# Weight sums of matmul pairs in one piece and in place, three buffers for split weights, and every pair's weights split two products ahead

## The chip, the core and the metric

The kernel runs on one core of one Trainium2 chip. The metric is the device time of one execution in microseconds (us). The engines are named as the profile names them: PE is TensorE's matmul, PEld its weight load, DVE VectorE, ACT ScalarE, POOL GpSimd, SP SyncE, which here only issues DMAs.

## The reference

The reference is one decoder layer on 512 prompt tokens and 8 sample tokens, 520 columns together, with a model width of 2048: adaLN modulation, two token mixers (mLSTM and forgetting attention), sigmoid gates that merge them, an output projection, and a feed-forward block with a causal convolution of width 3. Nearly all of its work is these dense products:

```python
h = modulate(rmsnorm(x, norm1_w), sh1, sc1)
... = jnp.split(h @ w_in + b_in, SPLIT_POINTS, axis=-1)
merged = jax.nn.sigmoid(ga) * (y_m @ w_proj_a) + jax.nn.sigmoid(gb) * (y_f @ w_proj_b)
x = x + g1 * (merged @ w_out)
h2 = modulate(rmsnorm(x, norm2_w), sh2, sc2)
a, g = jnp.split(h2 @ w_ffn_in, 2, axis=-1)
out = (jax.nn.gelu(conv(a)) * g) @ w_ffn_out
```

## The kernel before

Everything is float32 at the interface. A weight tile of 128 x 1024 is loaded into a buffer `raw` by SP (`wraw`, L158) and then split into two float32r tiles: `wh`, the rounded value, by a cast on ACT, and `wl`, the remainder, by a subtraction on DVE (`wtwo`, L167 to L177). The features are split in the same way into high and low. A product of weights and features is then three matmuls: high with high, high with low, low with high (`three_of`, L240).

Two kinds of stages use this. In a **dense stage** (`dense`, L205) one output chunk of 128 channels is computed with 48 or 96 matmuls, and the scheduler sets the order of the instructions by priorities. In a **pair stage** (`Pair`, L254 to L335) two output chunks and two halves of the 520 columns are computed together with seven products instead of eight, by sums of weight quarters and of feature quarters. A quarter is named by (output chunk, half of the 2048 inputs). Four products take a sum of quarters as weights; the sums are called 1 to 4 (`total`, L275): 1 is (1,0)+(1,1), 2 is sum 1 and (0,0), 4 is sum 2 and (0,1), 3 is (0,0) and (1,0). Each product is 24 matmuls of 128 x 128 weights with 260 columns and accumulates into a PSUM tile `x`, `y` or `z`. The products come in the order 1, 5, 6, 3, 7, 2, 4 (ORDER, L252), for the first pair of the output projection in the order 1, 3, 6, 5, 7, 2, 4 (ORDER1).

Pairs run in four stages: 11 pairs of gates and 4 of attention values (`GatePair`, `ValuePair`, about 530 to 835 us), 8 pairs of the output projection (`WoPair`, about 1320 to 1485), 41 of the feed-forward input (`FfnPair`, about 1580 to 2410) and 2 times 8 of its output (`FoPair`, from about 2490 and 2720). Around the last two stand a stage in which the features are made while the first weights run (about 1485 to 1580) and two stages `Whole` with plain products (about 2410 to 2490 and 2640 to 2720).

In a pair stage the program order is fixed on PE, DVE and ACT (`Ordered`, L53): `run_pairs` (L337) goes product by product. Before product number r of a pair it takes out the result of the product before, lets the pair make sums and splits for later products (`ahead(r)`, L303), lets the next pair do the same if its turn has come, and then issues the 24 matmuls. SP's loads run ahead of that order as far as buffers come free.

The buffers: 8 tiles `raw`; `wh` and `wl` with two tiles each in the pool `wp`, and from the end of the stage before the output projection a third each in the pool `cf`, which every third split takes (`turn`, `more`, L164 to L170). A sum of quarters lies in two tiles `sw` of 128 x 512 from the small pool `p` (`pt`, L93), so a sum is two additions and a split of a sum is two casts and two subtractions. With `early` 1 (the gate and value pairs) a quarter is split in two pieces as well, and a split stands one product ahead of its use; with `early` 2 (the other stages) a quarter is split in one piece and splits stand two products ahead. The adaLN sums are kept in a tile `ads` (`ada_out`, L421).

Of the kernel before, what the change touches and what calls it, by code (L numbers as in the profile page):

```python
# [63 lines left out]
def tile_hybrid_step(ctx: ExitStack, tc: tile.TileContext, I, O):  # L64
# [90 lines left out]
    def raw_tile():  # L155
        return wp.tile([P, 1024], F32, tag="raw", name=nm("raw"), bufs=8)

# [5 lines left out]

    turn = [0]  # L164
    more = []
# [12 lines left out]

    def wsplit(src, raw=None):
        with tc.high_priority():  # L180
            return wtwo([raw or wraw(src)], src.shape[1])

# [71 lines left out]
    class Pair:  # L254

        def __init__(self, rows, X, order, early):
            self.rows, self.X, self.order, self.early = rows, X, order, early
            self.w, self.s, self.made = {}, {}, []  # L260
            self.uses = {(0, 0): 3, (1, 0): 2, (0, 1): 2, (1, 1): 2, 1: 2, 2: 2, 3: 1, 4: 1}
# [4 lines left out]

        def pieces(self, x):
# [5 lines left out]
            return [u[:, :512] for u in t] if isinstance(x, int) else [t[:, :512], t[:, 512:]]  # L273

        def total(self, n):  # L275

            if n in self.made:
                return
            self.made.append(n)
            a, b = {1: ((1, 0), (1, 1)), 2: (1, (0, 0)), 4: ((0, 1), 2), 3: ((0, 0), (1, 0))}[n]  # L280
            out = []
            for u, v in zip(self.pieces(a), self.pieces(b)):
                t = pt("sw")
                V.tensor_tensor(t[:, :512], u, v, op=ALU.add)
                out.append(t)
            self.s[n] = out

        def split(self, n):
            src = {1: (0, 0), 2: (0, 1), 4: (1, 1), 5: 1, 6: 2, 3: 4, 7: 3}[n]
            whole = None if isinstance(src, int) or self.early == 1 else self.s[src]  # L290
            halves = self.pieces(src)
            self.w[n] = wtwo(halves if whole is None else [whole], 1024)

# [42 lines left out]

    def run_pairs(units, early, late, start=None):  # L337
        loads = {2: {1: ((0, 0),), 2: ((1, 0), (1, 1)), 5: ((0, 1),)},
                 1: {1: ((0, 0),), 3: ((1, 0), (1, 1)), 5: ((0, 1),)}}[early]
        for t in range(-early if start is None else start, 7 * len(units) + 5):  # L340
            u, r = divmod(t, 7)
            now, nxt = (units[v] if 0 <= v < len(units) else None for v in (u, u + 1))
            if 0 <= u - 1 < len(units):
                units[u - 1].after(r + 7)
            if now:
                if r > 0:
                    now.take(now.order[r - 1])
                now.ahead(r)
            if nxt:
                if r in loads and now:  # L350
                    nxt.load(*loads[r])
                if r >= 7 - early:
# [275 lines left out]
    square(1)  # L628
    turn[0] += 1
    w_first = [wp.tile([P, 1024], F32R, tag=t, name=nm(t)) for t in ("wh", "wl")]  # L630
# [98 lines left out]
    def next_group():  # L729
        if raws:  # L730
            raw, k = raws.pop(0)
            ready.append(wtwo([raw], k * NPH * P))

# [535 lines left out]
    class GatePair(Pair):  # L1269
        def __init__(self, gates):  # L1270
            self.gates = gates
            super().__init__([I["w_in"][49 + g] for g in gates], hX, ORDER, 1)

# [45 lines left out]
    class ValuePair(GatePair):  # L1319
        def __init__(self, heads):  # L1320
            self.heads = heads
            self.chunks = [25 + 3 * hh + 2 for hh in heads]
            Pair.__init__(self, [I["w_in"][i] for i in self.chunks], hX, ORDER, 1)

# [64 lines left out]
    run_pairs(units, 1, {}, 0)  # L1389
    hX = units = t = None  # L1390
# [411 lines left out]
    class WoPair(AddPair):  # L1802
        which = G1

        def __init__(self, c):
            super().__init__([I["w_out"][c + e] for e in range(2)], mX, ORDER if c else ORDER1, 2)
            self.c = c
# [57 lines left out]
    for n, j in enumerate(order):  # L1865
# [22 lines left out]
        if n == KC - 1:  # L1888
            more.append(cf)
            turn[0] = 0  # L1890
            with tc.high_priority():
                units[0].split(1)
                units[0].total(1)
                units[0].total(2)
                units[0].total(4)
                turn[0] = 2
                units[0].split(3)
# [29 lines left out]
    def parts2(u, o, e):  # L1927
        return wtwo([raws.pop((u, o, e))], 1024)

    def cast2(u, o, e):  # L1930

        turn[0] += 1
        wh, wl = ((cf if turn[0] % 3 == 0 else wp).tile([P, 1024], F32R, tag=t, name=nm(t)) for t in ("wh", "wl"))
        raw = raws.pop((u, o, e))
# [41 lines left out]
    def first_weights(o):  # L1976
# [3 lines left out]
    r2 = st("rr")  # L1980
    run_pairs(units, 2, {
        0: lambda: (m_sums(7, 0), m_sums(7, 1)), 1: lambda: (m_parts(7, 5), m_sums(7, 2)),
# [205 lines left out]
    class FfnPair(Pair):  # L2188
        def __init__(self, f):
            super().__init__((I["w_fi"][f], I["w_fi"][KF + f]), X, ORDER, 2)  # L2190
            self.f = f
# [27 lines left out]
    class Whole:  # L2219
# [21 lines left out]
        def split(self, c):  # L2241
            if c < KC:
                self.w[c] = wtwo([self.raw.pop(c)], NR * P)

# [114 lines left out]
    class FoPair(AddPair):  # L2359
        which = G2  # L2360

        def __init__(self, c, f0, fX):
            super().__init__([I["w_fo"][c + e][:, f0 * P:(f0 + 16) * P] for e in range(2)], fX, ORDER, 2)
            self.c, self.end = c, f0 + 16 == KF
# [66 lines left out]
    for k in range(0, KC, 2):  # L2431
# [7 lines left out]
    pairs1, pairs2 = units_of(whole[0], NR), units_of(whole[1], KF // 2 + NR)  # L2439
    run_pairs(units, 2, {-2: lambda: eight(2, 1, 1, (0, 1), w), -1: lambda: whole_copy(2),  # L2440
                         1: lambda: sum_parts(7), 2: lambda: whole_conv(2), 3: lambda: sum_parts(4),
                         4: lambda: whole_gate(2),
                         **g2, **whole[0].begin(7 * len(units))})
# [3 lines left out]
    units, last = pairs1  # L2447
    run_pairs(units, 2, {**rest_of(whole[0], units, last), **whole[1].begin(7 * len(units))})
    units, last = pairs2
    run_pairs(units, 2, rest_of(whole[1], units, last))  # L2450
    cf.release()
# [96 lines left out]
```

## Time and profile before

| | us |
|---|---|
| three timed runs | 2862.55, 2864.59, 2865.11 |
| their median | 2864.59 |
| the profiled execution: span from its first to its last instruction | 2875.7 |

The profiled execution gives no time besides its span; the span is 11.1 us (0.4%) longer than the median of the timed runs. All rows further down come from this one profiled execution, and positions in it are counted in us from its first instruction. In the page, "busy" is the time in which an engine had at least one instruction under way; matmuls overlap, so a busy PE need not be a PE at its peak.

### The profile page before, as it was taken

Reading aid. Unit: us, or ns where it says so; the run is one execution under the profiler, and the core shown is the slowest. Engines: PE = TensorE matmul, PEld = TensorE weight load, DVE = VectorE, ACT = ScalarE, POOL = GpSimd, SP = SyncE. Lnnn points to the kernel's source line nnn. Section 1 sums busy time; section 2 is a strip of 40 time slices with the busy share of each in tenths; the row PEclk is TensorE's granted clock in tenths of the full one; section 3 lists DMA queues with packets and bytes.
Section 4 is the critical chain, followed back from the end, with each engine's and each line's share of the span. In section 5 each row is a group of like instructions: output and inputs, shape, how many; then the busy total and the mean of one; then the engine's idle time right before and its main releaser. Section 6 shows DMA issues by size and latency. Waiting matters only on the chain.

```text
span 2875.7 us, 58597 instructions
## 1 busy us (share of the span) xinstructions
PE 2845.9 (99%) x23462; PEld 2734.9 (95%) x23462; DVE 2165.4 (75%) x4016; ACT 1379.1 (48%) x2451; POOL 363.6 (13%) x649
## 2 busy tenths in 40 slices
PE   8999999999999999999999999999999999999999
PEld 6899998999998989799999999999999999999999
DVE  5987754677855667368888888888888887787787
ACT  4346643455544554335555544444444445544543
POOL 0001101221101123302111000000000001100100
PEclk9999999999999999999999999999999999999999
DMA  9934458745456676657763444444443437746752
GB/s 340 313 130 142 141 164 300 246 151 170 148 166 222 208 243 231 209 186 230 221 202 104 128 137 144 144 138 151 135 152 114 149 111 201 191 153 186 204 159 89
DMA packets 214298, 514.23 MB, mean 179 GB/s; under 512 B 24512, under 2 KB 77232, under 8 KB 214024
## 3 DMA queue, kind: packets, MB, share of 16 engines
q1 hardware_dynamic: 177232, 416.07, 44.8%
q0 software_dynamic: 36352, 94.18, 10.9%
q8 instruction: 184, 3.01, 0.4%
q14 instruction: 90, 0.74, 0.1%
q10 hardware_dynamic: 440, 0.23, 0.0%
HBM read 440.47 MB, written 66.46 MB: 176 GB/s over the span
## 4 chain that ended last, share of the span: by engine, by line
PE 89%; issue 4%; DVE 3%; DMA 2%; ACT 2%; POOL 0%; SPq 0%; ACTq 0%; POOLq 0%; DVEq 0%
PE x L60 31%; PE y L60 16%; PE z L60 8%; PE fi L221 7%; PE gate L221 4%; PE fo L60 3%; PE pa L221 3%; PE pre L60 3%; PE mo L221 2%; PE adp L417 2%; PE mv L221 2%; PE adp L60 1%; DMA ar<-in_w_ada 1%; PE mq L221 1%; PE mk L221 1%
## 5 line engine op out<-in xcount | busy, mean ns | idle before, releaser
L60 ACT CAST wh<-sw 128x512 fp32r<-128x512 f32 x638 | 365.7, 621 | 246.2 <-PE z L60 74.2
L60 DVE TENSOR_TENSOR wl<-sw,wh 128x512 fp32r<-128x512 f32 x638 | 411.2, 686 | 86.8 <-ACT wh L60 83.9
L60 PE MATMUL x<-bf,wh 128*128 128x260 f32 x2624 | 475.9, 282 | 0.2 <-DVE tg L60 0.2
L60 ACT CAST wh<-raw 128x1024 fp32r<-128x1024 f32 (+2 forms) x350 | 316.7, 917 | 296.3 <-PE x L60 132.8
L60 DVE TENSOR_TENSOR wl<-raw,wh 128x1024 fp32r<-128x1024 f32 (+2 forms) x350 | 365.8, 1056 | 123.0 <-ACT wh L60 110.5
L60 PEld LDWEIGHTS x<-bf,wh 128*128 128x128 f32 x2624 | 403.4, 188 | 0.4 <-issue 0.4
L60 PE MATMUL x<-bf,wl 128*128 128x260 f32 x1312 | 369.8, 282 | 0.0
L176 DVE TENSOR_TENSOR wl<-raw,wh 128x1024 fp32r<-128x1024 f32 (+1 forms) x115 | 139.5, 1213 | 192.4 <-ACT wh L175 178.9
L60 PEld LDWEIGHTS x<-bf,wl 128*128 128x128 f32 x1312 | 246.9, 188 | 0.0
L60 PE MATMUL y<-bf,wh 128*128 128x260 f32 x1312 | 239.3, 283 | 0.0
L175 ACT CAST wh<-raw 128x1024 fp32r<-128x1024 f32 (+1 forms) x115 | 119.5, 1040 | 216.1 <-issue 42.9
L60 DVE TENSOR_TENSOR sw<-raw,raw 128x512 f32<-128x512 f32 x316 | 203.1, 683 | 0.0
L60 PEld LDWEIGHTS y<-bf,wh 128*128 128x128 f32 x1312 | 201.9, 188 | 0.0
L60 PE MATMUL x<-ff,wh 128*128 128x260 f32 x1024 | 186.5, 283 | 0.0
L60 PE MATMUL y<-bf,wl 128*128 128x260 f32 x656 | 185.1, 282 | 0.0
L60 PEld LDWEIGHTS x<-ff,wh 128*128 128x128 f32 x1024 | 157.8, 188 | 0.0
L60 PE MATMUL x<-ff,wl 128*128 128x260 f32 x512 | 144.6, 282 | 0.0
L60 PE MATMUL x<-hf,wh 128*128 128x260 f32 x720 | 131.4, 283 | 0.0
L60 PE MATMUL fo<-fe,wh 128*128 128x260 f32 x768 | 125.6, 284 | 1.6 <-DVE fo L60 1.1
L60 PEld LDWEIGHTS y<-bf,wl 128*128 128x128 f32 x656 | 123.4, 188 | 0.0
L60 PE MATMUL z<-bf,wh 128*128 128x260 f32 x656 | 120.3, 284 | 0.0
L60 PEld LDWEIGHTS x<-hf,wh 128*128 128x128 f32 x720 | 110.7, 188 | 0.0
(641 smaller groups left out, 7586.9 us busy)
## 6 DMA issues: line engine op xcount, KB each, us to landing
raw<-in_w_fi SPq DMA_DIRECT2D x176, 512.0 KB
raw<-in_w_in SPq DMA_DIRECT2D x155, 512.0 KB
ar<-in_w_ada SPq DMA_DIRECT2D x192, 256.0 KB
raw<-in_w_ada SPq DMA_DIRECT2D x96, 512.0 KB
raw<-in_w_fo SPq DMA_DIRECT2D x64, 512.0 KB
raw<-in_w_out SPq DMA_DIRECT2D x32, 512.0 KB
raw<-in_w_fo SPq DMA_DIRECT2D x32, 384.0 KB
dff<-cc POOLq DMA_DIRECT2D x44, 260.0 KB
```

Of the source, the lines that this page charges most:

```text
L60: return lambda *a, **k: self.tc.keep_in_program_order(getattr(self.eng, op)(*a, **k))
L175: S.copy(wh[:, o], t[:, :m])
L176: V.tensor_tensor(wl[:, o], t[:, :m], wh[:, o].bitcast(F32), op=ALU.subtract)
L221: T.matmul(acc[:, z, :HN], a[:, o], b[:, z * HN:(z + 1) * HN], start=(k == 0 and i == 0), stop=(k == K - 1 and i == 2))
L417: ins = T.matmul(ps[32 * g:32 * g + 32, :], cs[:, k, :], w, start=first, stop=last, tile_position=(0, 32 * g))
```

## The change

1. A sum of quarters is one addition of 128 x 1024 into one tile of the pool `raw`. Sum 3 is written over the quarter (1,0); with ORDER, sums 2 and 4 are written over the sum that they are made from. With ORDER1 sums 2 and 4 take a tile of their own, as sum 1 always does.
2. A split is one cast and one subtraction in every case. `wtwo` takes one tile instead of a list.
3. `wp` has three buffers of `wh` and of `wl` from the start; the third pair of tiles in `cf` and the counter `turn` go. `raw` has 7 buffers instead of 8, and a pair takes five of its tiles, four loads and sum 1, where it took four. Counted in matmuls of the two programs' order, from the last reading of a buffer to the first reading of the load that comes into it next: a load of the output projection or the feed-forward input had 204 or more before. With the change the quarter (1,1), which comes into the buffer of the sums of the pair before, has 76 to 85 in a running pair of these two stages, and the other three quarters 132 or more.
4. `early` goes: all pairs split two products ahead, and their loads stand where those with `early` 2 stood. In `ahead` a split stands before the sum of the same step, except sum 1.
5. `ads` comes from the pool `p` instead of a tile of its own. Two steps in the first feed-forward pairs (`whole_gate(2)` and `sum_parts(4)`) trade places.

```diff
-    wp = ctx.enter_context(tc.tile_pool(name="wp", bufs=2))
+    wp = ctx.enter_context(tc.tile_pool(name="wp", bufs=3))
...
-        return wp.tile([P, 1024], F32, tag="raw", name=nm("raw"), bufs=8)
+        return wp.tile([P, 1024], F32, tag="raw", name=nm("raw"), bufs=7)
...
-    def wtwo(tiles, n):
-
-        turn[0] += 1
-        wh, wl = ((more[0] if more and turn[0] % 3 == 0 else wp).tile([P, 1024], F32R, tag=t, name=nm(t))
-                  for t in ("wh", "wl"))
-        m = n // len(tiles)
-        for e, t in enumerate(tiles):
-            o = slice(e * m, (e + 1) * m)
-            S.copy(wh[:, o], t[:, :m])
-            V.tensor_tensor(wl[:, o], t[:, :m], wh[:, o].bitcast(F32), op=ALU.subtract)
+    def wtwo(raw, n=1024):
+
+        wh, wl = (wp.tile([P, 1024], F32R, tag=t, name=nm(t)) for t in ("wh", "wl"))
+        S.copy(wh[:, :n], raw[:, :n])
+        V.tensor_tensor(wl[:, :n], raw[:, :n], wh[:, :n].bitcast(F32), op=ALU.subtract)
         return wh, wl
...
-            a, b = {1: ((1, 0), (1, 1)), 2: (1, (0, 0)), 4: ((0, 1), 2), 3: ((0, 0), (1, 0))}[n]
-            out = []
-            for u, v in zip(self.pieces(a), self.pieces(b)):
-                t = pt("sw")
-                V.tensor_tensor(t[:, :512], u, v, op=ALU.add)
-                out.append(t)
-            self.s[n] = out
+            a, b = {1: ((1, 0), (1, 1)), 2: (1, (0, 0)), 4: (2, (0, 1)), 3: ((1, 0), (0, 0))}[n]
+            u, v = self.piece(a), self.piece(b)
+            t = u if n == 3 or self.order == ORDER and n != 1 else raw_tile()
+            V.tensor_tensor(t, u, v, op=ALU.add)
+            self.s[n] = t
...
-            if self.early == 2:
-                for n in {-2: (1,), -1: (2,), 0: (4,), 1: (3,)}.get(r, ()):
-                    self.total(n)
-            if r + self.early < 7:
-                self.split(self.order[r + self.early])
-            if self.early == 1:
-                for n in {-1: (1,), 0: (2,), 1: (4,), 2: (3,)}.get(r, ()):
-                    self.total(n)
+            if r == -2:
+                self.total(1)
+            if r + 2 < 7:
+                self.split(self.order[r + 2])
+            if r in (-1, 0, 1):
+                self.total((2, 4, 3)[r + 1])
...
-        loads = {2: {1: ((0, 0),), 2: ((1, 0), (1, 1)), 5: ((0, 1),)},
-                 1: {1: ((0, 0),), 3: ((1, 0), (1, 1)), 5: ((0, 1),)}}[early]
+        loads = {1: ((0, 0),), 2: ((1, 0), (1, 1)), 5: ((0, 1),)}
...
-        sb = cm.tile([P, 512], F32, tag="ads", name=nm("ads"))
+        sb = pt("ads")
...
         if j == KC - 2:
-            units[0].load((0, 0), (1, 0))
+            units[0].load((1, 0), (1, 1))
         if j == KC - 1:
-            units[0].load((1, 1), (0, 1))
+            units[0].load((0, 0), (0, 1))
...
             with tc.high_priority():
-                units[0].split(1)
-                units[0].total(1)
-                units[0].total(2)
+                units[0].ahead(-2)
+                units[0].ahead(-1)
...
-        wh, wl = ((cf if turn[0] % 3 == 0 else wp).tile([P, 1024], F32R, tag=t, name=nm(t)) for t in ("wh", "wl"))
+        wh, wl = (wp.tile([P, 1024], F32R, tag=t, name=nm(t)) for t in ("wh", "wl"))
```

How the instructions move shows at three places. The first is DVE in a pair of the feed-forward input, from the removal of `z` of the pair before to the split of product 7. Before:

```order
L60 TENSOR_TENSOR at_19920<-z_19779,tt_19804 128x260
L60 TENSOR_TENSOR sw_19987<-sw_19954,raw_19816 128x512
L60 TENSOR_TENSOR sw_19989<-sw_19956,raw_19816 128x512
L60 TENSOR_TENSOR wl_19992<-sw_19954,wh_19991 128x512
L60 TENSOR_TENSOR wl_19992<-sw_19956,wh_19991 128x512
L60 TENSOR_TENSOR sw_20021<-raw_19952,sw_19987 128x512
L60 TENSOR_TENSOR sw_20023<-raw_19952,sw_19989 128x512
L60 TENSOR_TENSOR wl_20026<-sw_19987,wh_20025 128x512
L60 TENSOR_TENSOR wl_20026<-sw_19989,wh_20025 128x512
```

And with the change, the same stretch:

```order
L60 TENSOR_TENSOR at_19357<-z_19223,tt_19248 128x260
L60 TENSOR_TENSOR wl_19423<-raw_19391,wh_19422 128x1024
L60 TENSOR_TENSOR raw_19391<-raw_19391,raw_19255 128x1024
L60 TENSOR_TENSOR wl_19452<-raw_19391,wh_19451 128x1024
L60 TENSOR_TENSOR raw_19391<-raw_19391,raw_19389 128x1024
L60 TENSOR_TENSOR wl_19486<-raw_19391,wh_19485 128x1024
L60 TENSOR_TENSOR raw_19289<-raw_19289,raw_19255 128x1024
```

Two instructions of half the width have become one each, the split stands before the sum of its step, and sums 2, 4 and 3 are written over one of their operands.

The second place is ACT at the head of the output projection, where the last dense chunk ends and the first pair (ORDER1) begins; `mf` are the feature parts of the merged mixers, `tt` the copy of a product's result. Before:

```order
L1736 CAST mf_16127<-sgm_14968 128x260
L1736 CAST mf_16131<-sgm_14968 128x260
L175 CAST wh_16267<-raw_16144 128x1024
L175 CAST wh_16283<-sw_16279 128x512
L175 CAST wh_16283<-sw_16281 128x512
L1710 CAST mf_16205<-sgm_15847 128x260
L1703 CAST mf_16291<-sgm_15108 128x520
L60 CAST wh_16324<-sw_16275 128x512
L60 CAST wh_16324<-sw_16277 128x512
L60 COPY tt_16364<-x_16337 128x260
```

And with the change:

```order
L167 CAST wh_15892<-raw_15769 128x1024
L1686 CAST mf_15742<-sgm_14593 128x520
L1686 CAST mf_15747<-sgm_15329 128x520
L1719 CAST mf_15752<-sgm_14593 128x260
L1719 CAST mf_15756<-sgm_14593 128x260
L167 CAST wh_15902<-raw_15900 128x1024
L1693 CAST mf_15830<-sgm_15472 128x260
L1686 CAST mf_15908<-sgm_14733 128x520
L60 CAST wh_15941<-raw_15898 128x1024
L60 COPY tt_15979<-x_15952 128x260
```

The cast for product 1 has moved ahead of four feature casts, and three split casts instead of five stand before the first copy.

The third place is SP, where the loads of adaLN weights `ar` for the last modulation begin to stand among the loads of the feed-forward input. Before, the first of them stand here:

```order
L161 DMA raw_20730<-in_w_fi 128x1024
L2409 DMA ar_20626<-in_w_ada 128x512
L161 DMA raw_20857<-in_w_fi 128x1024
L161 DMA raw_20893<-in_w_fi 128x1024
L2409 DMA ar_20580<-in_w_ada 128x512
L2409 DMA ar_20581<-in_w_ada 128x512
```

With the change the first of them stand further ahead, eight in a row, before the eleventh weight load of that stage (the tenth is the first row):

```order
L161 DMA raw_18491<-in_w_fi 128x1024
L2388 DMA ar_20006<-in_w_ada 128x512
L2388 DMA ar_20007<-in_w_ada 128x512
L2388 DMA ar_20008<-in_w_ada 128x512
L2388 DMA ar_20009<-in_w_ada 128x512
L2388 DMA ar_20971<-in_w_ada 128x512
L2388 DMA ar_20972<-in_w_ada 128x512
L2388 DMA ar_20973<-in_w_ada 128x512
L2388 DMA ar_20974<-in_w_ada 128x512
L161 DMA raw_18620<-in_w_fi 128x1024
```

Eight loads of `ar` stand ahead of the eleventh weight load of the stage and of all later ones.

## Rows read from the trace of the kernel before

**Rows 1.** The page's first part: busy time and instructions of each engine.

```profile
span 2875.7 us, 58597 instructions
PE 2845.9 (99%) x23462; PEld 2734.9 (95%) x23462; DVE 2165.4 (75%) x4016; ACT 1379.1 (48%) x2451; POOL 363.6 (13%) x649
```

**Rows 2.** The page's second part: GB/s moved, in 40 slices of the span.

```profile
GB/s 340 313 130 142 141 164 300 246 151 170 148 166 222 208 243 231 209 186 230 221 202 104 128 137 144 144 138 151 135 152 114 149 111 201 191 153 186 204 159 89
```

**Rows 3.** The chain of work that ended last, shares by engine.

```profile
PE 89%; issue 4%; DVE 3%; DMA 2%; ACT 2%; POOL 0%; SPq 0%; ACTq 0%; POOLq 0%; DVEq 0%
```

**Rows 4.** Busy time by stretch: length, engines (instructions), granted clock, DMA share, GB/s.

```profile
530.00:820.00 290.00, 290.00 (x2428) 290.00 (x2428) 225.17 (x387) 151.03 (x301) 47.77 (x90) 1.00 0.51 166
1140.00:1160.00 20.00, 17.38 (x100) 15.11 (x99) 12.19 (x18) 2.79 (x3) 11.96 (x11) 0.84 0.73 239
1320.00:1480.00 160.00, 159.51 (x1329) 159.11 (x1329) 137.57 (x263) 89.05 (x148) 31.70 (x50) 1.00 0.76 232
1580.00:2410.00 830.00, 830.00 (x6903) 815.23 (x6903) 688.34 (x1135) 398.12 (x651) 70.10 (x202) 1.00 0.42 139
2490.00:2640.00 150.00, 150.00 (x1252) 150.00 (x1251) 126.23 (x230) 65.64 (x107) 8.15 (x15) 1.00 0.51 163
```

**Rows 5.** Whom PE waited for: us in total, times, longest.

```profile
PE gate L221 <- issue: 4.0, 9, 0.7
...
PE fa L60 <- ACT bf L60: 1.1, 1, 1.1
PE fo L60 <- DVE fo L60: 1.1, 6, 0.2
PE fa L60 <- DVE bf L60: 0.8, 2, 0.6
PE fa L60 <- DVE wl L60: 0.6, 1, 0.6
...
PE y L60 <- ACT tt L60: 0.5, 1, 0.5
...
PE x L60 <- DVE tg L60: 0.2, 1, 0.2
```

**Rows 6.** Instructions by line and shape: count, busy us, mean ns, idle before.

```profile
L60 DVE TENSOR_TENSOR wl<-sw,wh 128x512 fp32r<-128x512 f32 x638 | 411.2, 686 | 86.8 <-ACT wh L60 83.9 <-PE fo L60 2.8
L60 DVE TENSOR_TENSOR wl<-raw,wh 128x1024 fp32r<-128x1024 f32 x221 | 269.8, 1221 | 100.2 <-ACT wh L60 99.7
L60 DVE TENSOR_TENSOR sw<-raw,raw 128x512 f32<-128x512 f32 x316 | 203.1, 683 | 0.0
...
L60 ACT CAST wh<-sw 128x512 fp32r<-128x512 f32 x638 | 365.7, 621 | 246.2 <-PE z L60 74.2 <-PE x L60 71.3 <-DVE wl L60 56.1
L60 ACT CAST wh<-raw 128x1024 fp32r<-128x1024 f32 x221 | 232.2, 1051 | 208.1 <-PE x L60 103.2 <-PE y L60 68.2 <-PE pre L60 12.5
```

**Rows 7.** In order of time, a feed-forward pair: start, us, engine, instruction.

```profile
1703.70 1.14 ACT L60 CAST wh<-sw 128x512 fp32r<-128x512 f32 x2 [1.83 <-DVE wl L60]
...
1705.33 1.28 DVE L60 TENSOR_TENSOR wl<-sw,wh 128x512 fp32r<-128x512 f32 x2
...
1709.31 0.40 PE L60 MATMUL y<-bf,wh 128*128 128x260 f32 x2
```

**Rows 8.** The chain in order of time, same pair: one product of 24 matmuls.

```profile
1712.37 2.87 PE x L60 x24
```

**Rows 9.** In order of time, a gate pair.

```profile
700.82 1.29 DVE L60 TENSOR_TENSOR wl<-sw,wh 128x512 fp32r<-128x512 f32 x2 [0.44 <-ACT wh L60]
...
702.39 0.41 PE L60 MATMUL x<-hf,wh 128*128 128x260 f32 x2
```

**Rows 10.** In order of time, head of the output projection, ACT and then PE.

```profile
1330.79 0.36 ACT L60 COPY tt<-y 128x260 f32<-128x260 f32 x1
...
1331.20 0.51 PE L60 MATMUL y<-mf,wh 128*128 128x260 f32 x2 [0.49 <-ACT tt L60]
```

**Rows 11.** The DMA view, 1710 to 1720 us: GB/s in 40 slices of 0.25 us.

```profile
GB/s 0 0 0 0 0 82 147 279 328 377 393 328 426 344 246 295 360 279 213 131 33 0 0 0 0 0 0 0 0 0 0 0 0 0 0 164 82 197 344 360
```

More of the change, by code (lines that the diff above doesn't have):

```diff
@@ L180, in wsplit @@
         with tc.high_priority():
-            return wtwo([raw or wraw(src)], src.shape[1])
+            return wtwo(raw or wraw(src), src.shape[1])
     def on(f, *a):
@@ L254, in tile_hybrid_step, with __init__ @@
     class Pair:
-        def __init__(self, rows, X, order, early):
-            self.rows, self.X, self.order, self.early = rows, X, order, early
+        def __init__(self, rows, X, order):
+            self.rows, self.X, self.order = rows, X, order
             self.w, self.s, self.made = {}, {}, []
@@ L265, in load, with piece @@
                 self.s[i, j] = wraw(self.rows[i][:, j * 1024:(j + 1) * 1024])
-        def pieces(self, x):
+        def piece(self, x):
             t = self.s[x]
@@ L272, in pieces @@
                 del self.s[x]
-            return [u[:, :512] for u in t] if isinstance(x, int) else [t[:, :512], t[:, 512:]]
+            return t
         def total(self, n):
@@ L279, in total @@
             self.made.append(n)
-            a, b = {1: ((1, 0), (1, 1)), 2: (1, (0, 0)), 4: ((0, 1), 2), 3: ((0, 0), (1, 0))}[n]
-            out = []
-            for u, v in zip(self.pieces(a), self.pieces(b)):
-                t = pt("sw")
-                V.tensor_tensor(t[:, :512], u, v, op=ALU.add)
-                out.append(t)
-            self.s[n] = out
+            a, b = {1: ((1, 0), (1, 1)), 2: (1, (0, 0)), 4: (2, (0, 1)), 3: ((1, 0), (0, 0))}[n]
[3 more added lines that the diff above has]
+            self.s[n] = t
         def split(self, n):
             src = {1: (0, 0), 2: (0, 1), 4: (1, 1), 5: 1, 6: 2, 3: 4, 7: 3}[n]
-            whole = None if isinstance(src, int) or self.early == 1 else self.s[src]
-            halves = self.pieces(src)
-            self.w[n] = wtwo(halves if whole is None else [whole], 1024)
+            self.w[n] = wtwo(self.piece(src))
         def product(self, n):
@@ L335, in temp, with run_pairs @@
             return st(name)
-    def run_pairs(units, early, late, start=None):
-        loads = {2: {1: ((0, 0),), 2: ((1, 0), (1, 1)), 5: ((0, 1),)},
-                 1: {1: ((0, 0),), 3: ((1, 0), (1, 1)), 5: ((0, 1),)}}[early]
-        for t in range(-early if start is None else start, 7 * len(units) + 5):
+    def run_pairs(units, late, start=-2):
+        loads = {1: ((0, 0),), 2: ((1, 0), (1, 1)), 5: ((0, 1),)}
+        for t in range(start, 7 * len(units) + 5):
             u, r = divmod(t, 7)
@@ L351, in run_pairs @@
                     nxt.load(*loads[r])
-                if r >= 7 - early:
+                if r >= 5:
                     nxt.ahead(r - 7)
@@ L731, in next_group @@
             raw, k = raws.pop(0)
-            ready.append(wtwo([raw], k * NPH * P))
+            ready.append(wtwo(raw, k * NPH * P))
     ready = [w_first]
@@ L1271, in __init__ @@
             self.gates = gates
-            super().__init__([I["w_in"][49 + g] for g in gates], hX, ORDER, 1)
+            super().__init__([I["w_in"][49 + g] for g in gates], hX, ORDER)
         def temp(self, name):
@@ L1322, in __init__ @@
             self.chunks = [25 + 3 * hh + 2 for hh in heads]
-            Pair.__init__(self, [I["w_in"][i] for i in self.chunks], hX, ORDER, 1)
+            Pair.__init__(self, [I["w_in"][i] for i in self.chunks], hX, ORDER)
         def out(self, e):
@@ L1388, in tile_hybrid_step @@
             hX[n][i] = parts_of(t)
-    run_pairs(units, 1, {}, 0)
+    run_pairs(units, {}, 0)
     hX = units = t = None
@@ L1805, in __init__ @@
         def __init__(self, c):
-            super().__init__([I["w_out"][c + e] for e in range(2)], mX, ORDER if c else ORDER1, 2)
+            super().__init__([I["w_out"][c + e] for e in range(2)], mX, ORDER if c else ORDER1)
             self.c = c
@@ L1888, in tile_hybrid_step @@
         if n == KC - 1:
-            more.append(cf)
-            turn[0] = 0
             with tc.high_priority():
@@ L1895, in tile_hybrid_step @@
                 units[0].total(4)
-                turn[0] = 2
                 units[0].split(3)
@@ L2362, in __init__ @@
         def __init__(self, c, f0, fX):
-            super().__init__([I["w_fo"][c + e][:, f0 * P:(f0 + 16) * P] for e in range(2)], fX, ORDER, 2)
+            super().__init__([I["w_fo"][c + e][:, f0 * P:(f0 + 16) * P] for e in range(2)], fX, ORDER)
             self.c, self.end = c, f0 + 16 == KF
@@ L2439, in tile_hybrid_step @@
     pairs1, pairs2 = units_of(whole[0], NR), units_of(whole[1], KF // 2 + NR)
-    run_pairs(units, 2, {-2: lambda: eight(2, 1, 1, (0, 1), w), -1: lambda: whole_copy(2),
-                         1: lambda: sum_parts(7), 2: lambda: whole_conv(2), 3: lambda: sum_parts(4),
-                         4: lambda: whole_gate(2),
+    run_pairs(units, {-2: lambda: eight(2, 1, 1, (0, 1), w), -1: lambda: whole_copy(2),
+                         1: lambda: sum_parts(7), 2: lambda: whole_conv(2), 3: lambda: whole_gate(2),
+                         4: lambda: sum_parts(4),
                          **g2, **whole[0].begin(7 * len(units))})
@@ L2447, in tile_hybrid_step @@
     units, last = pairs1
-    run_pairs(units, 2, {**rest_of(whole[0], units, last), **whole[1].begin(7 * len(units))})
+    run_pairs(units, {**rest_of(whole[0], units, last), **whole[1].begin(7 * len(units))})
     units, last = pairs2
-    run_pairs(units, 2, rest_of(whole[1], units, last))
+    run_pairs(units, rest_of(whole[1], units, last))
     cf.release()
```

12 lines of the change are left out of this document (4 added, 8 removed).

## The prediction

> **What bounds the kernel now.** I read the page's totals first. PE is busy for 2845.9 of 2875.7 us [rows 1], so at most 29.8 us lie in gaps, and a change that leaves every matmul in place can win only from those gaps or from the spacing of the matmuls. The chain that ended last agrees: 89% of it is PE, DVE and ACT together are 5% [rows 3]. DVE is busy 75% of the span, yet a busy share does not say who waits, so I went to the stretches one by one.
>
> In the pair stages, which the change rewrites, PE has no gap: 290.00 of 290.00 us with gate and value pairs, 830.00 of 830.00 with feed-forward pairs, 150.00 of 150.00 with output pairs; the output projection has 159.51 of 160.00 [rows 4]. The spacing is 290.00/2428 = 119.4 ns, 830.00/6903 = 120.2 ns, 150.00/1252 = 119.8 ns. A product of 24 matmuls takes 2.87 us [rows 8], a pair of seven 20.1 us.
>
> Then I asked whom PE waited for. Behind the start-up the list has few lines [rows 5]: 4.0 us in `gate`, put down to "issue" (no semaphore of another engine), 2.5 us where the feed-forward features are made (`fa`), 1.1 us in a stage of plain products (`fo`). Only two belong to pairs: `y` 0.5 us and `x` 0.2 us, each once, at the head of a stage. So 0.7 us is all that earlier splits can win from waits.
>
> **What the change costs and saves, part by part.**
>
> *One piece instead of two.* 320 sums and 365 splits lose one instruction each. Two halves end to end take 1.28 us on DVE [rows 7], one piece 1.221 [rows 6]: DVE saves 685 x 0.06 = 41 us. By the means of single halves, 2 x 0.686 against 1.221, it would be 685 x 0.15 = 103 us; I take the 41, because that row is a pair as it really ran. ACT saves 365 x (1.14 - 1.051) = 32 us [rows 6, 7]. Half a microsecond of DVE per pair, all beside PE that did not wait: 0 on the path.
>
> The one piece also ends later than the first half did, for a reader that needs only the first quarter of the weights. No such reader waits here: in the feed-forward pair the subtraction that starts at 1705.33 and takes 1.28 us ends at 1706.61, and its product starts at 1709.31, a margin of 2.70 us [rows 7]. Cast and subtraction can no longer overlap by halves: 1.05 + 1.22 = 2.27 us for both in a row, against 0.62 + 1.28 = 1.90 [rows 6, 7]. That costs 0.37 us of a margin of 2.70: nothing. If the margin went, the price would be up to 0.37 us in four splits of a pair.
>
> *In place.* Sum 2 over sum 1 must wait until the cast and the subtraction of product 5 have read sum 1. The subtraction stands right ahead of it on DVE, and it waits for that same cast. No new wait on another engine arises; what is queued behind is the next subtraction, with the 2.3 us just found. 0.
>
> *Gate and value pairs a product earlier.* Here the margin is thin: a subtraction starts at 700.82, takes 1.29 us, ends at 702.11, and its product starts at 702.39, 0.28 us later [rows 9]. With splits two products ahead the margin grows by one product, 2.87 us. But PE did not wait: 290.00 of 290.00. A margin that was never overdrawn is worth 0.
>
> *Head of the output projection.* PE waits 0.49 us at 1331.20 for the ACT copy that began at 1330.79 [rows 10]. The order shows why: five split casts stand between feature casts and that copy, with the change three, the first of them further ahead. Bounds: 0 (the copy still comes last, since it needs `x`) and 0.7 with the feed-forward head. I take 0.5.
>
> *`ads` in another pool, two steps traded, `early` gone.* No instruction more; nothing in the rows of pair stages waits there. 0.
>
> *Seven buffers, five tiles a pair.* This is the part that speaks against the change. The load of the quarter (1,1) now has 76 to 85 matmuls between the freeing of its buffer and its reader, where it had 204: 76 x 0.1195 = 9.1 us instead of 24.4. What a load needs: at 1711.25 to 1715.0 us two of them (1 MB) pass in 3.75 us [rows 11]; at the 313 to 340 GB/s of the start [rows 2] it would be 3.1 to 3.4, and in the output projection, the busiest pair stage with 0.76 of the DMA engines and 232 GB/s [rows 4], twice the 3.75 if other traffic took half, 7.5. All below 9.1. Should sum 1 come late, DVE holds the split of product 1 behind it, which is due two products later: 2 x 2.87 - 1.22 - 1.22 = 3.3 us more. So PE is reached when a load lands over 12.4 us after its buffer was freed. I take 0; bounds 0 and rival C. The eight `ar` loads now in a row are 2 MB, about 6.5 us at those rates, once, ahead of loads with over 9 us: 0.
>
> *A rule against the sum.* The trace shows 119.4 ns at a DVE share of 225.17/290 = 78% and 119.8 ns at 126.23/150 = 84% [rows 4], the granted clock 1.00 (the 2.4 GHz level) in both. The Trainium skill, "TensorE: Matmul & The Clock Gate", section "Wait — 56ns, not 53.3ns?", says that warm matmuls follow each other at N / 2.4 GHz plus about 2.5 ns; for 260 columns that is an estimate of 110.8 ns, and this trace does not agree. What fills the rest no row tells; were it traffic of the other engines, a change that relieves DVE would win, which is rival D.
>
> **Sum.** 2875.7 - 0.5 = 2875.2 us for the profiled execution. That execution stands 11.1 us above the median of the timed runs, 2864.59; against the median the forecast is 2864.1.
>
> **Rivals.**
>
> *B, faster: the one bad stretch dissolves.* Between 1140 and 1160 us, in a dense gate stage, only 100 matmuls ran in 20 us, where 168 would fit at 0.119: some 8 us lost, 2.62 of them idle, the granted clock at 0.84, a mix of the 2.4 and 1.2 GHz levels [rows 4]. The Trainium skill, same page, Part 1, says that the clock depends on how active PE was; the trace agrees, with 0.84 where PE idled and 1.00 in the other stretches of rows 4. "Issue" instead of a semaphore [rows 5] says that no data was late, which speaks against a cure by earlier splits. But dense stages get a third buffer for splits from the start, SP's order and the timing of all traffic around it move, and so the stall may not recur: 2864.1 - 8 = 2856.
>
> *C, slower: the quarter (1,1) comes late.* Place: the eight pairs of the output projection; it decides above 12.4 us from a buffer's freeing to its load's landing. At 1 us a pair 8 x 1 = 8 us: 2872. In the feed-forward stage, with 0.42 of the DMA engines busy [rows 4], it is far less likely; 41 pairs at 0.2 us, the size of the smaller pair wait of rows 5, would give the same 8. Against it: the longest landing that I can argue is 7.5.
>
> *D, a little faster: the spacing follows DVE.* From the rows of the rule, 0.4 ns for 6 points of share. DVE loses 41 of some 1600 us of pairs, 2.6 points, so 0.17 ns x 13,440 matmuls = 2.3 us: 2861.8. Against it: the feed-forward stage has the widest spacing at 688.34/830 = 83%, no more than the 84% of the output pairs.
>
> *E, slower: the bad stretch doubles.* The same retiming as in B makes a second one, +8: 2872.
>
> *F, the change is not what it says.* If sums stayed in halves nothing would move, 2864.6; the order shows them 1024 wide.
>
> **How the numbers follow.** Chances: the forecast 0.62, B 0.18, C 0.09, D 0.04, E 0.06, F 0.01. A measurement of this kernel can tell about 0.2%, 5.7 us, from no change: 2858.9 to 2870.3 is "same". That takes in the forecast, D and F, 0.67; faster is B, 0.18; slower C and E, 0.15. Cases inside "same" hold less than 8 in 10, so the range reaches to B and, on the other side, to C and E, half a microsecond beyond each: 2855.5 to 2872.5.
>
> **What would show it right or wrong.** Right: DVE at about 2165 - 41 = 2124 us and ACT at about 1379 - 32 = 1347 with PE still near 2846; sums and splits 128 x 1024 at about 1.22 us each; spacing 119 to 120 ns in the pair stretches; the `y` wait of 0.5 gone; the gate pair's margin at about 3 us, with no gain from it; 20 us from one feed-forward pair to the next. Wrong: PE waiting for `wl`, or for DVE behind a load, in a pair stretch (C); spacing below 119 ns (D); or the 1140 to 1160 stretch changed by several us (B, E). The prediction as a whole is wrong if the pair stages take another time, since its core is that they were bound by matmuls alone.

## The result, and the profile after

| | us |
|---|---|
| the kernel before, 20 runs beside it: median (lowest to highest) | 2864.50 (2862.16 to 2866.05) |
| the changed kernel, 20 runs | 2869.19 (2866.78 to 2874.41) |
| ratio, 95% interval | 1.0017 (1.0010 to 1.0023) |
| profiled execution: span, and its own time | 2866.7, 2868.39 |

The change costs 4.7 us, 0.17%. The time lies inside the range of the forecast, but the whole interval of the ratio lies above 1, where the forecast was 0.5 us faster. Further down, two runs that stand far apart from all others, 8518 us of e13 at a granted clock of 0.31 and 4605 us of the kernel before at 0.56, are left out of ratios and ranges.

The first part of the page of the changed kernel, which answers to [rows 1], and the shares of the chain, to [rows 3]:

```profile
span 2866.7 us, 57603 instructions
PE 2835.1 (99%) x23462; PEld 2729.0 (95%) x23462; DVE 2125.7 (74%) x3331; ACT 1343.7 (47%) x2086; POOL 383.5 (13%) x649
...
PE 87%; DVE 5%; DMA 4%; ACT 2%; issue 1%; POOL 0%; SPq 0%; ACTq 0%; DVEq 0%; POOLq 0%
```

DVE is busy 39.7 us less and ACT 35.4, near what was reckoned (41 and 32), and none of it shows in the time. The span is shorter than the 2875.7 of before, although the runs are longer: the profiled execution of before was no typical one (first experiment). The same stretches as in [rows 4], of the changed kernel:

```profile
530.00:820.00 290.00, 290.00 (x2429) 290.00 (x2429) 215.36 (x232) 140.62 (x200) 47.08 (x89) 1.00 0.51 165
1140.00:1160.00 20.00, 19.60 (x163) 19.18 (x162) 15.56 (x26) 7.05 (x8) 13.15 (x14) 1.00 0.87 290
1320.00:1480.00 160.00, 157.48 (x1302) 156.05 (x1300) 133.57 (x202) 84.19 (x116) 29.40 (x47) 1.00 0.76 236
1580.00:2410.00 830.00, 830.00 (x6928) 817.40 (x6927) 666.74 (x822) 385.22 (x499) 90.98 (x201) 1.00 0.43 139
```

The gate and value pairs run at 290.00/2429 = 119.4 ns a matmul, as before. In the window of the output projection PE is idle for 2.5 us, against 0.5 in [rows 4], but after its stall of 12 us (first experiment) the profile of before stands at another place of the program there: in a second profile of before the same window has 2.0 us. What that stage lost is counted further down, matmul by matmul. The waits of PE, which answer to [rows 5]:

```profile
PE x L60 <- DVE tg L60: 2.0, 1, 2.0
...
PE x L60 <- ACT tg L60: 0.7, 1, 0.7
...
PE pa L213 <- ACT pao L1356: 0.6, 1, 0.6
...
PE x L60 <- DVE wl L60: 0.3, 2, 0.2
PE fy L1187 <- DVE fpl L225: 0.3, 1, 0.3
PE fPT L1477 <- DVE rt L1416: 0.3, 1, 0.3
```

The `y` wait of 0.5 is gone, and the `x` wait for `tg` at the head of the feed-forward input has grown from 0.2 to 2.0 us. Two groups of instructions on DVE and one on ACT, from the view by line and shape, say what the pairs do now, and answer to [rows 6]:

```profile
L60 DVE TENSOR_TENSOR wl<-raw,wh 128x1024 fp32r<-128x1024 f32 x583 | 711.5, 1221 | 296.4 <-ACT wh L60 293.9 <-PE y L60 1.4
L60 DVE TENSOR_TENSOR raw<-raw,raw 128x1024 f32<-128x1024 f32 x315 | 384.4, 1220 | 5.4
```

```profile
L60 ACT CAST wh<-raw 128x1024 fp32r<-128x1024 f32 x583 | 611.3, 1049 | 730.6 <-DVE raw L60 386.2 <-PE z L60 127.9 <-issue 76.8
```

One piece takes 1.22 us, as foreseen. The two engines now wait for each other: DVE's subtractions 294 us for ACT's casts, ACT's casts 386 us for DVE's sums. Before, the list of waits had 194 us for the first, where it now has 311, and 26 us for the second:

```profile
DVE wl L60 <- ACT wh L60: 194.4, 286, 4.0
...
ACT wh L60 <- DVE sw L60: 25.5, 19, 2.3
```

The timeline of a feed-forward pair of the changed kernel shows it, ACT first, then DVE (start, duration, idle time before and whose end it was):

```profile
1700.07 1.05 ACT L60 CAST wh<-raw 128x1024 fp32r<-128x1024 f32 x1 [2.63 <-DVE raw L60]
...
1703.73 1.05 ACT L60 CAST wh<-raw 128x1024 fp32r<-128x1024 f32 x1 [1.16 <-DVE raw L60]
...
1707.26 1.05 ACT L60 CAST wh<-raw 128x1024 fp32r<-128x1024 f32 x1 [1.50 <-DVE raw L60]
```

```profile
1701.15 1.23 DVE L60 TENSOR_TENSOR wl<-raw,wh 128x1024 fp32r<-128x1024 f32 x1 [1.20 <-ACT wh L60]
1702.41 1.23 DVE L60 TENSOR_TENSOR raw<-raw,raw 128x1024 f32<-128x1024 f32 x1
1704.81 1.23 DVE L60 TENSOR_TENSOR wl<-raw,wh 128x1024 fp32r<-128x1024 f32 x1 [1.17 <-ACT wh L60]
1705.95 1.22 DVE L60 TENSOR_TENSOR raw<-raw,raw 128x1024 f32<-128x1024 f32 x1
```

Cast (1700.07), subtraction (1701.15), sum (1702.41), cast (1703.73), subtraction, sum, cast (1707.26): one round takes 3.66 and 3.53 us, where a product takes 2.87 [rows 8]. So a split falls some 0.7 us further behind with each product, for three products of a pair, and catches up in the rest, which need no sums. Traced tile by tile (first matmul with a `wl` less the end of its subtraction), the margins of one pair run 3.52, 2.73, 1.96, 1.29, 1.95, 2.68, 2.94 us; before they were 2.9 to 3.6 throughout. In the middle of a stage 1.29 us is enough. At its head, where other work fills DVE and ACT as well, it is not. The order comes with the overwriting: a sum that is written over its operand has to stand behind the split that still reads this operand. Before, the sum had tiles of its own and stood ahead of the split of its step.

### The profile page after: what moved, and what is told of

Its sections match the earlier page's. It is cut to its first block, busy times and chain, and to the rows that moved or that the text cites. A ratio compares the mean times of both kernels' runs of the same rounds, so it can differ in the third digit from the quotient of the medians.

```text
span 2866.7 us, 57603 instructions
## 1 busy us (share of the span) xinstructions
PE 2835.1 (99%) x23462; PEld 2729.0 (95%) x23462; DVE 2125.7 (74%) x3331; ACT 1343.7 (47%) x2086; POOL 383.5 (13%) x649
## 4 chain that ended last, share of the span: by engine, by line
PE 87%; DVE 5%; DMA 4%; ACT 2%; issue 1%; POOL 0%; SPq 0%; ACTq 0%; DVEq 0%; POOLq 0%
PE x L60 31%; PE y L60 15%; PE z L60 8%; PE fi L213 5%; PE fo L60 4%; PE gate L213 3%; PE pb L213 3%; PE pa L213 3%; PE mo L213 2%; PE pre L60 2%; PE mv L213 2%; DMA ar<-in_w_ada 2%; DMA raw<-in_w_in 1%; PE adp L402 1%; DVE wl L60 1%
## 5 line engine op out<-in xcount | busy, mean ns | idle before, releaser
L60 ACT CAST wh<-raw 128x1024 fp32r<-128x1024 f32 (+1 forms) x624 | 645.3, 1035 | 738.4 <-DVE raw L60 386.2
L60 DVE TENSOR_TENSOR wl<-raw,wh 128x1024 fp32r<-128x1024 f32 (+1 forms) x624 | 750.5, 1203 | 313.6 <-ACT wh L60 310.5
L60 DVE TENSOR_TENSOR raw<-raw,raw 128x1024 f32<-128x1024 f32 x315 | 384.4, 1220 | 5.4
L168 DVE TENSOR_TENSOR wl<-raw,wh 128x1024 fp32r<-128x1024 f32 x116 | 141.8, 1223 | 171.0 <-ACT wh L167 166.5
L167 ACT CAST wh<-raw 128x1024 fp32r<-128x1024 f32 x116 | 121.7, 1049 | 218.0 <-DMA raw<-in_w_in 42.7
L213 PE MATMUL fi<-hh,wh 128*128 128x260 f32 x512 | 109.3, 295 | 0.0
L60 PEld LDWEIGHTS fo<-fe,wh 128*128 128x128 f32 x768 | 105.5, 188 | 3.9 <-DVE fo L60 2.5
```

The lines of the kernel that those rows point to most:

```text
L60: return lambda *a, **k: self.tc.keep_in_program_order(getattr(self.eng, op)(*a, **k))
L167: S.copy(wh[:, :n], raw[:, :n])
L168: V.tensor_tensor(wl[:, :n], raw[:, :n], wh[:, :n].bitcast(F32), op=ALU.subtract)
L213: T.matmul(acc[:, z, :HN], a[:, o], b[:, z * HN:(z + 1) * HN], start=(k == 0 and i == 0), stop=(k == K - 1 and i == 2))
```

## The experiments

Each time is a median, and each ratio is against runs of the kernel before in the same series. There were three series, e1 to e5, e6 to e9 and e10 to e13, with medians of before of 2865.18, 2865.43 and 2865.30 us.

To find places, I compared the start of the same matmul, counted in PE's order, in two profiled executions: how much longer a stretch between two such matmuls took than in the second profile of before (e1). Position in that profile, and difference in us (`pa` is the product of the mLSTM mixer with its projection, `adp` a sum of adaLN products, made in eight groups of 16 matmuls along the feed-forward input):

| stretch | changed | again (e9) | e5 | e6 | e10 | e7 | e8 | e12 |
|---|---|---|---|---|---|---|---|---|
| 181 to 233, dense | +0.8 | +0.8 | +0.8 | +0.8 | +0.8 | 0 | +0.8 | 0 |
| 448 to 544, `pa` | +0.9 | 0 | 0 | 0 | +0.2 | 0 | 0 | 0 |
| 957 to 1106, dense | +2.7 | +3.2 | +4.2 | +4.3 | +4.5 | +1.8 | +3.0 | 0 |
| 1312 to 1326, head of the output projection | -0.6 | -0.6 | -0.8 | -0.8 | -0.6 | 0 | -0.9 | 0 |
| 1326 to 1470, its pairs | +1.3 | +1.3 | -0.1 | -0.1 | +0.8 | 0 | -0.1 | 0 |
| 1470 to 1510, its end | +1.3 | -0.1 | -0.2 | -0.2 | 0 | -0.1 | +1.2 | -0.2 |
| 1566 to 1572, feed-forward head | +1.8 | +3.3 | +1.8 | +0.3 | +3.2 | 0 | 0 | 0 |
| three `adp` groups | -3.2 | -3.2 | -3.2 | -3.2 | -3.2 | -1.9 | -2.5 | -3.2 |

A column is one execution, and some of them stand off their medians (e10 by 3.3 us, e9 by 1.5). The row 1470 to 1510 is no effect of the change: the same program has +1.3 and -0.1 there.

**e1, the kernel before again.** No edit.

> The kernel before, unchanged, for a second profile. If the stall of 12 us between 1140 and 1207 us belonged to that one execution, the span is about 2863 us, the granted clock of 1140 to 1160 us is 1.00 and some 168 matmuls run in it; the three `adp` groups of 3.2 us in the feed-forward stage come again. If the stall belongs to the kernel, the span is again near 2875 us.

Measured, one run: 2864.3 us, span 2862.6. The stall did not come again:

```profile
1140.00:1160.00 20.00, 19.47 (x161) 19.03 (x160) 14.18 (x24) 6.90 (x10) 10.81 (x12) 1.00 0.84 274
```

161 matmuls at a granted clock of 1.00, against 100 at 0.84 [rows 4]. Between 1140 and 1207 us the same matmuls take 11.9 us less than in the first profile. The stall belonged to one execution, and with it went the ground of rivals B and E: there was nothing in the median to dissolve.

**e2, the trade of two steps undone.**

```diff
-                         1: lambda: sum_parts(7), 2: lambda: whole_conv(2), 3: lambda: whole_gate(2),
-                         4: lambda: sum_parts(4),
+                         1: lambda: sum_parts(7), 2: lambda: whole_conv(2), 3: lambda: sum_parts(4),
+                         4: lambda: whole_gate(2),
```

> The changed kernel with whole_gate(2) and sum_parts(4) back in the old order. Theory 1 (eight low parts of 2.8 us now stand on DVE ahead of `tg`, for which the first feed-forward pair waits 2.0 us): that wait falls to about 0.2 us and the time to about 2867.4, ratio 1.0010. Rival (the wait comes from later loads or splits at that place): no change, 2869.2, ratio 1.0017.

Measured: 2867.29 us, ratio 1.0009 (1.0000 to 1.0018), just as Theory 1 has it, and yet the theory falls: the wait for `tg` is still there in full.

```profile
PE x L60 <- DVE tg L60: 2.0, 1, 2.0
```

The time alone would have misled. The 1.9 us are not from this place, and they are not shown to be a difference at all: the interval overlaps that of the changed kernel, and e9 gave 1.0013 without any edit.

**e3, the third pair of split buffers for pairs only.**

```diff
-    wp = ctx.enter_context(tc.tile_pool(name="wp", bufs=3))
+    wp = ctx.enter_context(tc.tile_pool(name="wp", bufs=2))
...
+        if more and turn[0] % 3 == 0:
+            return [wp.tile([P, 1024], F32R, tag=t + "3", name=nm(t), bufs=1) for t in ("wh", "wl")]
+        return [wp.tile([P, 1024], F32R, tag=t, name=nm(t)) for t in ("wh", "wl")]
...
+            more.append(1)
+            turn[0] = 0
             with tc.high_priority():
                 units[0].ahead(-2)
```

> The changed kernel, but the third pair of split buffers is used only in the stages of pairs and after them, as the dense stages had two before. Theory 2 (a split that stands a chunk earlier is queued on ACT and DVE ahead of work that PE waits for): the waits at 184 us (0.5), in `pa` (0.9) and before `fy` (2.4) go, 2869.2 - 3.8 = 2865.4, ratio 1.0003. Rival (seven buffers for loads make the dense stages late): the waits stay, 2869.2.

Measured: 2872.30 us, ratio 1.0025 (1.0015 to 1.0035), slower. The loss at 181 us shrank to 0.3 and the one at 957 to 1106 stayed at 2.4, so Theory 2 holds for the first place at best. Losses came at the first gate pair (1.4) and at the head of the output projection (1.3), where the third pair joins only then. Its profiled execution is 5.3 us above the median; one wait of 4.1 us for `sc`, a tile of the sample tokens' attention, at 1157 us is part of that. Another 2.7 us against e1 along the feed-forward pairs I did not follow up.

**e5, sums taken out of the chain in the output projection.** Sum 2 gets a tile `sx`, sum 4 goes over sum 1, and the sum stands ahead of the split.

```diff
+            spare = getattr(self, "spare", None) and self.order == ORDER
             t = u if n == 3 or self.order == ORDER and n != 1 else raw_tile()
+            if spare and n == 2:
+                self.t1, t = u, self.spare()
+            if spare and n == 4:
+                t = self.__dict__.pop("t1")
...
+            spare = hasattr(self, "spare")
...
+            if spare and r in (-1, 0, 1):
+                self.total((2, 4, 3)[r + 1])
             if r + 2 < 7:
                 self.split(self.order[r + 2])
-            if r in (-1, 0, 1):
+            if not spare and r in (-1, 0, 1):
                 self.total((2, 4, 3)[r + 1])
```

> The changed kernel, but in the output projection sum 2 has a tile of its own, sum 4 is written over sum 1, and the sum stands ahead of the split of its step. Theory 3 (cast, subtraction and sum in place form one chain of 3.5 us a product against 2.87 us of PE, so the margin of a split falls by 0.7 us a product): the margins stay near 2 us, the waits at 1346 and 1367 us (0.9 and 0.3) go, 2869.2 - 1.2 = 2868.0. Rival (the loads are late there, or ACT is held by its own work): waits and time as in the changed kernel.

Measured: 2865.06 us, ratio 0.9999 (0.9990 to 1.0009). The waits in the pairs of the output projection went: 1326 to 1470 us is 1.4 us shorter than in the changed kernel, near the 1.2 I had seen in the list. The median is 4.1 us lower; where the rest of that lies the table does not show. Smallest margins are still near 0 at the first pair, so "near 2" held only from the second on. One of the waits shows how far a late sum reaches: in the changed kernel a cast of ACT waits for its sum, an ACT table load and a copy that frees `x` stand behind it, and PE waits 0.74 us for the copy.

```profile
1343.27 1.05 ACT L60 CAST wh<-raw 128x1024 fp32r<-128x1024 f32 x1 [2.21 <-DVE raw L60]
1344.34 1.28 ACT L60 ACT_TABLE_LOAD   x1
1345.63 0.38 ACT L60 COPY tg<-x 128x260 f32<-128x260 f32 x1
```

**e6, the same in the feed-forward input too,** and e13, e6 again.

> As e5_spare, and in the feed-forward input too. Theory 3 (one chain of cast, subtraction and sum in place, 3.5 us a product against 2.87): DVE stands 1.8 us earlier at the first pair of that stage, the wait for `tg` falls from 2.0 to about 0.2 us, the margins of a split stay near 3 us instead of falling to 1.3, and the time is 1.8 us below e5_spare, ratio 0.9993. Rival (the wait for `tg` comes from the low parts of the features alone): the wait stays at 2.0 us, ratio 0.9999.

> e6_spare_ffn once more, for a second profile and a second interval: ratio 0.9993, margins in the feed-forward pairs near 3.2 us, the wait for `tg` at most 0.6 us.

Measured: 2863.24 us, ratio 0.9993 (0.9984 to 1.0002), and 2863.36, 0.9995 (0.9985 to 1.0004). The wait for `tg` fell to 0.5 us, where about 0.2 was expected:

```profile
PE x L60 <- DVE tg L60: 0.5, 1, 0.5
```

The subtractions of a steady pair no longer follow a sum; they come one every 2.88 us, a product of PE, and their mean margin rose from 2.6 to 3.4 us (3.5 before):

```profile
1700.34 1.23 DVE L60 TENSOR_TENSOR wl<-raw,wh 128x1024 fp32r<-128x1024 f32 x1 [0.83 <-ACT wh L60]
1703.22 1.23 DVE L60 TENSOR_TENSOR wl<-raw,wh 128x1024 fp32r<-128x1024 f32 x1 [0.99 <-ACT wh L60]
1706.10 1.23 DVE L60 TENSOR_TENSOR wl<-raw,wh 128x1024 fp32r<-128x1024 f32 x1 [0.59 <-ACT wh L60]
```

**e10, the own tile, but the split ahead of the sum.** The edit is shown against e6.

```diff
-            spare = hasattr(self, "spare")
+            spare = False
```

> As e6_spare_ffn (sum 2 in a tile of its own in the output projection and the feed-forward input), but the split of a step again ahead of its sum, as in the changed kernel. If the order on DVE makes the chain (the sum stands behind the subtraction, which waits for the cast), the own tile helps nothing: waits for `tg` of 2.0 us, margins falling to 1.3 us, ratio 1.0013. If the overwriting makes it, it is as e6_spare_ffn, ratio 0.9993.

Measured: 2866.04 us, ratio 1.0004 (0.9995 to 1.0013); between the two. The waits are those of the changed kernel: 1.9 us for `tg`, and margins down to 1.5 us on average in their lowest place (1.3 in the changed kernel, 3.1 in e6). So the order on DVE makes the chain, also where sum 2 overwrites nothing. The time says less: e13, in the same series, is 2.7 us faster, and the runs of the two do not overlap, which prices the order, with the tile at hand; but e9 is another 2.7 us slower than e10, in another series, and the pairs and the two heads in the table give 0.6 of that. What an overwritten tile costs beyond the order stays open.

```profile
PE x L60 <- DVE tg L60: 1.9, 1, 1.9
```

**e7, the kernel before with seven load buffers,** and **e8, with all buffers of the changed one.**

```diff
-        return wp.tile([P, 1024], F32, tag="raw", name=nm("raw"), bufs=8)
+        return wp.tile([P, 1024], F32, tag="raw", name=nm("raw"), bufs=7)
```

> The kernel before with seven load buffers and nothing else. If the seventh buffer less is what changes the order of the dense stage between 957 and 1106 us, the 2.5 us that the changed kernel loses there appear here, 2864.5 + 2.5 = 2867.0, ratio 1.0009. If not, ratio 1.0000 and that stretch as before. Late loads (rival C) would show as waits for `raw` in pair stages: none expected with four tiles a pair.

> The kernel before with all the buffers of the changed one (seven for loads, three for splits everywhere, `ads` in the other pool), sums and splits of pairs as before. If the buffers make the loss in dense stages: 0.8 us at 181 to 233 us and 2.5 us at 957 to 1106 us, no wait for `tg` at the first feed-forward pair and the `y` wait of 0.5 at the output projection still there: 2864.5 + 3.3 = 2867.8, ratio 1.0012. If the sums and splits make it: ratio 1.0000.

Measured: 2863.54 us, 0.9993 (0.9984 to 1.0003), and 2863.44, 0.9995 (0.9986 to 1.0004). The loss between 957 and 1106 us appears in both, 1.8 and 3.0 us; as a count, 1199 matmuls of before (e1) and 1184 with seven load buffers:

```profile
957.00:1106.00 149.00, 148.03 (x1184) 131.16 (x1183) 95.18 (x218) 74.11 (x148) 31.46 (x31) 1.00 0.69 232
```

In e8, as in the changed kernel, PE's order is another at 56 matmuls of that stretch, where `fi` and `fy`, two tiles of that stage, are placed differently. In e7 PE's order is that of before, matmul for matmul; there PE waits 0.6 us for `rt` and 0.4 us for `fpl`, two tiles of DVE for which e1 has no wait. What makes them late is not shown. Neither kernel is slower than before, for both win back at `adp` most of what they lose in dense stages. e8 stands beside e9 and has all its buffers, but the old sums, splits and loads of pairs: it is 5.3 us faster. So buffers are not what made the change slow.

**e9, the changed kernel again.**

> The changed kernel once more, beside the others and for a second profile. The wait for `tg` (2.0 us) and the three `adp` groups of 1.9 us instead of 3.2 should come again if they belong to the program; the 0.9 us in `pa` should vary. Ratio 1.0017 by the first measurement; e2_trade_back, whose program differs in one trade that changed no wait, gave 1.0009, so 1.0013 is as likely.

Measured: 2868.76 us, ratio 1.0013 (1.0004 to 1.0022). The wait for `tg` came again (2.0), and so did the short `adp` groups; the 0.9 us in `pa` did not. The same wait cost more this time. The 4 us behind it, in the changed kernel's first profile and then in e9:

```profile
1573.44:1577.44 4.00, 4.00 (x33) 4.00 (x34) 3.97 (x5) 1.06 (x1) 0.00 (x0) 1.00 0.16 64
```

```profile
1573.83:1577.83 4.00, 4.00 (x21) 4.00 (x22) 3.97 (x5) 1.05 (x1) 0.00 (x0) 0.58 0.16 66
```

After PE had idled for 2.0 us, the granted clock stayed at 1.00 in one execution and was 0.58 in the other, near its lower level (1.2 of 2.4 GHz): 21 matmuls instead of 33, and the head cost 3.3 us instead of 1.8. e10 is like e9 (0.62); e2, e3 and e5 are like the first.

**e12, the kernel before with earlier `ar` loads.**

```diff
-        g2.update({t + 1: on(g2_load, k), t + 2: on(g2_load, k + 1), t + 5: on(g2_product, k)})
+        g2.update({t - 2: on(g2_load, k), t - 1: on(g2_load, k + 1), t + 5: on(g2_product, k)})
```

> The kernel before, with the `ar` loads of the last modulation issued three products earlier. Theory 4 (three `adp` groups of the feed-forward input take 3.2 instead of 1.9 us since their loads land late; the changed kernel wins this back because its `ar` loads stand earlier on SP): the groups take 1.9 us, 2864.5 - 3.2 = 2861.3, ratio 0.9989. Rival (the longer groups have to do with PE's own order): groups and time unchanged, ratio 1.0000.

Measured: 2860.84 us, ratio 0.9985 (0.9976 to 0.9994): faster than both kernels, by 4.5 us than the one before in the same runs. The first group, in e1 and then in e12:

```profile
1644.72 2.88 PE L60 MATMUL adp<-ar,cs 128*32 128x512 f32 x16
```

```profile
1644.72 1.92 PE L60 MATMUL adp<-ar,cs 128*32 128x512 f32 x16
```

In e1 the last seven `ar` loads are issued from 1635.26 on for 4.57 us, and a load of that kind takes 6.1 us to land (median of the changed kernel's page); the product starts at 1644.72. The waits of the weight loads between 1566 and 2410 us name it, in e1; the changed kernel, e9 and e12 have no such line:

```profile
PEld adp L60 <- DMA ar<-in_w_ada: 3.2, 8, 1.0
```

## Why the prediction was right and wrong

- **What bounds the kernel: right in the steady pairs, too wide as a sentence.** 119.4 ns in the gate and value pairs, before and after. "Bound by matmuls alone" failed in the first pairs of two stages and at three `adp` groups: the feed-forward stretch, 830.00 of 830.00 us busy, hid over 3 us of late loads. The 120.2 ns that I read from it is 119.8 without them (e12).
- **One piece instead of two: right.** 1.22 us each, DVE -39.7, ACT -35.4 us, nothing on the path.
- **"In place. [...] No new wait on another engine arises; what is queued behind is the next subtraction, with the 2.3 us just found. 0." This is the step that failed.** I priced one split, 1.05 + 1.22 against a margin of 2.70, and asked whether a wait was new. I did not follow the loop: the next cast needs the sum, the sum stands behind this subtraction, and this subtraction needs this cast. A round is 1.05 + 1.22 + 1.22 = 3.5 us by rows 6, if an addition of 128 x 1024 takes as long as the subtraction of that shape. That is more than the 2.87 of rows 8, so the margin had to fall by 0.6 us a product; it fell by 0.7 to 0.8. None of my rivals held this. The change's own order rows had shown it: the split ahead of the sum. e6 against e9, which stood beside each other, prices it: 2868.76 - 2863.24 = 5.5 us, and e8, which keeps the old sums and splits, gives 5.3. By places the profiles show 2.9 us of it (first profile) or 4.4 (e9, with the clock's fall): 1.4 in the pairs of the output projection, 1.5 or 3.0 at the feed-forward head. The rest I could not place.
- **Gate and value pairs earlier: 0, right,** but the margin is not about 3 us: it starts at 3.5 and falls to 1.3, the chain again.
- **Head of the output projection: 0.5 won, right in size** (-0.6), and given back by the chain in the second and third pair (+1.3). The reason, three split casts instead of five, is not shown: e8 still splits the sums in halves, has no `y` wait either, and wins 0.9.
- **Seven buffers, five tiles: 0 in the pairs, right.** Loads land in 4.0 us (feed-forward) and 4.6 us (output projection), medians of the page, against 9.1; 315 sums waited 5.4 us in all, so rival C is out. For the dense stages my sum had no term at all; with seven buffers alone they lost 1.8 us, with all buffers of the change 3.8 (0.8 and 3.0).
- **The eight `ar` loads: "0" was wrong in our favour.** I asked what they delay, not who waits for them. Three `adp` groups were 1.0 to 1.3 us too long; e12 wins 4.5 us with that alone, somewhat more than the 3.2 of its profile.
- **The other rivals.** B and E rested on one execution, 11 us above the median; I noted that difference and did not ask where it lay. D is out: DVE fell from 78% to 74% of the gate stretch and the spacing stayed at 119.4 ns. In the feed-forward stretch e12, with DVE as busy as before, runs as many matmuls (6930) as the changed kernel (6928):

```profile
1580.00:2410.00 830.00, 829.94 (x6930) 817.14 (x6930) 687.68 (x1138) 400.50 (x659) 72.55 (x205) 1.00 0.44 141
```

- **The size of it.** Chain 5.5 us (e6 against e9), buffers and `ar` together -2.0 (e8, an interval that takes in 0): 3.5, against 4.7 and 3.3 us (e9) measured. That the range held 2869.2 was luck: it reached up there for C and E, and neither came.

## What to carry to other kernels

Where two engines hand work to each other, add up one whole round of the hand-over in the order in which the queues hold it, and compare it with the time that the third engine gives per step; a margin for one step says nothing on a loop that is longer than the step. Here the lost margin was paid in the first pairs of two stages, where other work stood in the queues of DVE and ACT as well. And look into the profiled execution's distance from the median before a rival is built on one of its stretches; a few microseconds of a run's time can agree with a theory whose wait is still there.

## What the runs showed of the hardware

- A PE stall of 12 us, with a granted clock of 0.84 from 1140 to 1160 us, came in one execution of the kernel before and not in its next. A wait for `sc` in that stretch was 0.4 to 4.1 us in the twelve other profiles.
- After a wait of PE of 1.9 to 2.1 us at one and the same place, the granted clock over the next 4 us was 1.00 in four profiles (the changed kernel, e2, e3, e5) and 0.58 and 0.62 in two (e9, e10), where the place cost about 1.5 us more.
- A group of 16 `adp` matmuls took 1.92 us with its loads issued early, and 2.88 to 3.19 in three groups of each profile of before, where they came late. The list of PE's own waits shows none of it, and PE counts as busy throughout; the list of the weight loads' waits has it, 3.2 us. It was found by comparing the same matmuls in two traces.
- The spacing of matmuls did not follow DVE's work: 119.4 ns with 225.17 and with 215.36 us of DVE in 290, and 119.8 ns with 687.68 and with 666.74 in 830.
